# Moving four on-chip buffers from byte 16512 to a multiple of 4 KiB, in a kernel bound by its DMA engines

## Chip, cores, metric

One core of a Trainium2 chip. The metric is device time in microseconds (us) of one execution, the median of several. The profile's span, from the first to the last instruction, is some 1.4 us shorter than the time.

## The reference

```python
def setup_inputs():
    return {"x": np.random.randn(8192, 8192).astype(np.float32)}

def reference(x):
    a, b = np.split(x, 2, axis=-1)
    return a * (1 / (1 + np.exp(-b)))
```

268 MB are read and 134 MB written; each output needs one sigmoid and one product.

## The kernel before

The work goes through 32 tiles of 256 rows. Each of 128 partitions takes two adjacent rows (R = 2), so a partition's share of a load is one run of 65,536 bytes in HBM and on chip, and of a store one run of 32,768 bytes. Two input slots and two output slots take turns. Loads are issued by SyncE, stores by ScalarE; the sigmoid runs on ScalarE (ACT) in place, the product on VectorE (DVE).

```python
    pool = ctx.enter_context(tc.tile_pool(name="io", bufs=1))
    xs = [pool.tile([P, R * n_cols], fp32, name=f"x_sb{k}") for k in range(SLOTS)]
    os = [pool.tile([P, R * half], fp32, name=f"o_sb{k}") for k in range(SLOTS)]
    # ...
    for i in range(n_tiles):
        # ...
        rows = xs[i % SLOTS].rearrange("p (r h m) -> p r h m", r=R, h=2)
        packed = os[i % SLOTS].rearrange("p (r m) -> p r m", r=R)
        load = nc.sync.dma_start(out=xs[i % SLOTS], in_=x_t[i])
        # ... the first and last tile are worked in four parts, the others in one
        def store(cols):
            ins = nc.scalar.dma_start(out=out_t[i, :, cols], in_=os[i % SLOTS][:, cols])
            now["stores"].append(ins)
        for k, (r, c) in enumerate(parts):
            b = rows[:, r, 1, c]
            sig = nc.scalar.activation(out=b, in_=b, func=SIG)
            mul = nc.vector.tensor_mul(out=packed[:, r, c], in0=rows[:, r, 0, c], in1=b)
            # ... dependencies that follow from others are taken out
        store(chunks[-1] if i == n_tiles - 1 else slice(0, R * half))
```

The buffers are laid out one after another behind 16 KiB of scratch and four small constants. As built, they begin at bytes 16512, 82048, 147584 and 180352 of each partition.

## Time and profile before

| | before |
|---|---|
| time, median (range) | 933.2 us (933.03 to 933.31) |
| span of the profile | 931.7 us |
| DVE busy, ACT busy | 30%, 24% |
| DMA engines | full in all 40 slices, 432 GB/s |

To read such a page: look for the row that is full everywhere. Here it is the DMA row alone, and a change has to shorten what the DMA engines do, or it does nothing. The prediction below shows the lines.

This document also uses the records of single DMA packets, which the trace holds with start, duration, size and queue. A recorded duration is 3 to 4 ns longer than the time from one start to the next on the same engine; both forms occur below and are named.

### The profile page before, as it was taken

The numbers are of one execution on the slowest core, as the hardware profiler recorded it, in microseconds if no ns is written. First come the engines' busy times: TensorE is split into PE (matmuls) and PEld (weight loads), VectorE is DVE, ScalarE is ACT, GpSimd is POOL, SyncE is SP. The second block draws the span as 40 slices with busy tenths as digits, with TensorE's granted clock in tenths as the row PEclk, the third lists the DMA queues.
The fourth block names the chain that finished last, engine by engine and source line by source line (L and its number), as shares of the span: only waits on it lengthen the run. The fifth ranks groups of instructions, "written<-read, shape, count | busy, mean of one in ns | idle before, by whom it ended". The sixth has DMA issues, their size and how long they took to land.

```text
span 931.7 us, 247 instructions
## 1 busy us (share of the span) xinstructions
DVE 278.7 (30%) x38; ACT 227.1 (24%) x39; POOL 0.2 (0%) x4
## 2 busy tenths in 40 slices
DVE  0333213333133331233312333123331233312333
ACT  1323330233311333113331133311333113332033
POOL 0000000000000000000000000000000000000000
DMA  9999999999999999999999999999999999999999
GB/s 405 428 450 428 422 456 405 450 428 428 450 418 438 428 436 442 428 428 450 447 408 428 442 459 428 413 460 411 450 428 425 453 408 447 428 428 450 425 430 405
DMA packets 9649, 402.67 MB, mean 432 GB/s; under 512 B 1072, under 2 KB 1072, under 8 KB 1072
## 3 DMA queue, kind: packets, MB, share of 16 engines
q1 hardware_dynamic: 4608, 268.44, 66.6%
q10 hardware_dynamic: 5040, 134.22, 33.4%
q14 instruction: 1, 0.01, 0.0%
HBM read 268.44 MB, written 134.22 MB: 432 GB/s over the span
## 4 chain that ended last, share of the span: by engine, by line
DMA 73%; DVE 15%; ACT 12%; issue 0%; ACTq 0%
DMA x_sb<-in_x_dram 73%; DVE o_sb L69 15%; ACT x_sb L68 12%; ACTq L62 0%; ACTq L68 0%
## 5 line engine op out<-in xcount | busy, mean ns | idle before, releaser
L69 DVE TENSOR_TENSOR o_sb<-x_sb 128x8192 f32<-128x8192 f32 (+1 forms) x38 | 278.7, 7344 | 647.1 <-ACT x_sb L68 647.1
L68 ACT ACTIVATE x_sb<-x_sb 128x8192 f32<-128x8192 f32 (+1 forms) x38 | 225.8, 5952 | 695.6 <-DMA x_sb<-in_x_dram 694.4
L68 ACT ACT_TABLE_LOAD x1 | 1.3, 1283 | 0.8 <-PEq L188 0.8
L188 POOL MEMSET const-bfloat16-1.0<- 128x1 bf16 x1 | 0.1, 102 | 0.0
L188 POOL MEMSET const-uint8-127<- 128x1 uint8 x1 | 0.1, 102 | 0.0
L188 POOL MEMSET const-float32-0.0<- 128x1 f32 x1 | 0.1, 99 | 0.2 <-issue 0.2
L188 POOL MEMSET const-float32-1.0<- 128x1 f32 x1 | 0.1, 99 | 0.0
## 6 DMA issues: line engine op xcount, KB each, us to landing
out_dram<-o_sb ACTq DMA_DIRECT2D x31, 4096.0 KB, 34.7
out_dram<-o_sb ACTq DMA_DIRECT2D x4, 1024.0 KB, 5.6
x_sb<-in_x_dram SPq DMA_DIRECT2D x32, 42.2
```

The lines of the kernel that those rows point to most:

```text
L68: sig = nc.scalar.activation(out=b, in_=b, func=SIG)
L69: mul = nc.vector.tensor_mul(out=packed[:, r, c], in0=rows[:, r, 0, c], in1=b)
L188: nc = _bacc.Bacc("TRN2", target_bir_lowering=False, num_devices=1)
```

## The change

Its intent: DMA transfers might run faster when each partition's run begins on a round address, so a filler tile is put ahead of the four buffers.

```diff
     pool = ctx.enter_context(tc.tile_pool(name="io", bufs=1))
+    start = -(-nc.sbuf_base // 32) * 32
+    pool.tile([P, -start % (1 << 12) // 4], fp32, name="below")
     xs = [pool.tile([P, R * n_cols], fp32, name=f"x_sb{k}") for k in range(SLOTS)]
     os = [pool.tile([P, R * half], fp32, name=f"o_sb{k}") for k in range(SLOTS)]
```

The filler has 3968 bytes per partition. 16512 is 128 past a multiple of 256; the new start 20480 is 5 x 4096.

## The prediction

> **What bounds the kernel now.** I read the page first, then the DMA view, the table of stages, the waits of the load queue, the groups by shape and the chain of waits in order of time, and last the records of single DMA packets.
>
> The page shows two compute engines that idle most of the time and DMA engines that never do:
>
> ```profile
> span 931.7 us, 247 instructions
> DVE 278.7 (30%) x38; ACT 227.1 (24%) x39; POOL 0.2 (0%) x4
> DMA  9999999999999999999999999999999999999999
> DMA packets 9649, 402.67 MB, mean 432 GB/s; under 512 B 1072, under 2 KB 1072, under 8 KB 1072
> q1 hardware_dynamic: 4608, 268.44, 66.6%
> q10 hardware_dynamic: 5040, 134.22, 33.4%
> ```
>
> The DMA row is 9 in all 40 slices, and the shares of the two queues (loads on q1, stores on q10) add up to 100%. The table of stages says the same of two-tile stretches in the steady part and of the end (columns: stretch, busy time of DVE, ACT and POOL, clock, DMA share, GB/s):
>
> ```profile
> 102.88:160.84 57.96, 17.39 (x2) 14.06 (x3) 0.00 (x0) 1.00 1.00 432
> 160.84:218.77 57.93, 17.38 (x2) 14.06 (x2) 0.00 (x0) 1.00 1.00 434
> 914.71:931.70 16.99, 8.99 (x4) 7.54 (x4) 0.00 (x0) 1.00 0.94 401
> ```
>
> DMA share is 1.00 while DVE works 17.4 us and ACT 14.1 us of 58. Only in the last 17 us is a small part of the transfer time open.
>
> The chain of waits seems to tell another story, with compute on it:
>
> ```profile
> 102.88 7.04 ACT x_sb L68
> 109.94 8.70 DVE o_sb L69
> 118.66 42.09 DMA x_sb<-in_x_dram
> 160.84 7.04 ACT x_sb L68
> ```
>
> Each load waits for the multiplication that frees its slot. But the 15.7 us of ACT and DVE lie beside the other slot's load and the store before, as the share of 1.00 shows. A faster multiplication would only let a load enter the full queue earlier, and its 42 us would grow by as much. So the bound is the time that each DMA engine needs for its own packets.
>
> **What one packet costs.** The page counts 5040 + 4608 packets; the packet records show what they are: per load 128 of 65,536 bytes and 16 of 4 bytes (one per engine, the completion), per whole store 128 of 32,768 bytes and 16 of 4, per quarter store at the end 128 of 8,192 and 16 of 4. Following packets on one engine (each starts 3 to 4 ns before the recorded end of the last, so I lined them up by that), the time from one start to the next has hardly any spread: 2414.2 ns for a load packet, 1209.4 for a whole store packet, 305.9 for a quarter one, and 5.9 for a 4-byte one.
>
> The skill's page gives 32 bytes at 850 MHz per engine, 27.2 bytes per ns or 1.176 ns a beat. At that rate the data alone take 65,536/27.2 = 2409.4, 32,768/27.2 = 1204.7, 8,192/27.2 = 301.2 and one beat 1.2 ns. What is left is 4.8, 4.7, 4.7 and 4.7 ns: four beats, whatever the size, direction and kind.
>
> Sum for one of 16 engines: 256 x 2414.2 + 248 x 1209.4 + 32 x 305.9 + 67 x 5.9 ns = 618.0 + 299.9 + 9.8 + 0.4 = 928.1 us. The span is 931.7, so all that is not packets is 3.6 us: the start until the first load packet, the longer first packets and the gaps at the end.
>
> **What the Trainium skill says.** "DMA: Bandwidth & Descriptors", section "Where 436 GB/s comes from", has 16 ports x 256 bits x 850 MHz = 435.2 GB/s. The trace agrees: 432 over the span, so 99%. At 435.2 the 402.67 MB take 925.3 us (an estimate from that page's rate and this page's bytes), the least that any change of this kind can reach: 6.4 us or 0.7% below the profiled span.
>
> The same page, "How a descriptor splits into AXI transactions", is what the change bets on: a piece that does not start on a multiple of 256 bytes has its first transaction start at the boundary below, and the bytes before the start are fetched for nothing. Byte 16512 is 64 x 256 + 128, so a read from there would fetch 128 needless bytes, four beats of 32. That is exactly the excess found above, which makes the bet tempting. The section tells of reads alone; a store reads SBUF, a load writes it.
>
> The same page, "Why small descriptors are slow (HBM only)", has a rival for those four beats: a fixed overhead of about 3 cycles per packet on the engine's internal bus. The trace shows 4 for all four sizes. That includes the 4-byte completion packets, which move none of the tiles' data. I take this as the better fit: one cause explains all.
>
> "SBUF — State Buffer", section "Operand start alignment", asks only for a multiple of the element size and says that its runs timed nothing. So no page gives a speed for 4 KiB alignment.
>
> **The change part by part.** Removed: nothing. Added: a tile that no instruction reads or writes; it holds 3968 bytes per partition, costs no time, and still fits. Moved: the four buffers begin at 20480, 86016, 151552 and 184320 in place of 16512, 82048, 147584 and 180352, all higher by 3968. I compared the instructions of before and after engine by engine: same rows, same order, same shapes; only line and buffer numbers differ. Tile sizes and addresses in HBM stay.
>
> Distances between buffers stay too (65,536 and 32,768 bytes), so nothing that depends on how two buffers lie to one another can change.
>
> Compute: no gain, and it would not count.
>
> ```profile
> L69 DVE TENSOR_TENSOR o_sb<-x_sb 128x8192 f32<-128x8192 f32 x30 | 260.8, 8692 | 608.1 <-ACT x_sb L68 608.1
> L68 ACT ACTIVATE x_sb<-x_sb 128x8192 f32<-128x8192 f32 x30 | 210.9, 7031 | 652.8 <-DMA x_sb<-in_x_dram 652.8
> L69 DVE TENSOR_TENSOR o_sb<-x_sb 128x2048 f32<-128x2048 f32 x8 | 17.9, 2288 | 39.0 <-ACT x_sb L68 39.0
> L68 ACT ACTIVATE x_sb<-x_sb 128x2048 f32<-128x2048 f32 x8 | 14.8, 1903 | 42.9 <-DMA x_sb<-in_x_dram 41.6 <-DVE o_sb L69 0.9 <-issue 0.3
> ```
>
> From 2048 to 8192 columns DVE grows by 6404 ns for 6144 columns, 1.042 ns each, and ACT by 5128, 0.835 each; taken back to no columns both leave about 0.15 to 0.2 us. A straight line through both sizes shows no step an address could remove, and in the steady part both hide.
>
> Transfers: under the fixed-overhead reading all periods stay, so the sum stays 928.1 us and the change is 0. Sum of the parts: 0 us.
>
> **The rivals.** First, wasted beats at both ends of both directions: every data packet loses its four beats. 256 + 248 + 32 = 536 packets per engine x 4 x 1.176 ns = 2.5 us, all on the bound, giving 930.7 us (-0.27%). For it: the excess is four beats. Against it: 4-byte packets show the same four, and would need a second cause. Second, the store side only: 280 x 4.7 ns = 1.3 us, giving 931.9. Against it: loads and stores would then show different excesses unless something else adds four beats to loads; they show 4.8 and 4.7. Third, a slowdown, if a 4 KiB boundary makes all streams begin on the same place in the memory. Against it: the distances were multiples of 4 KiB before. To cross 2% it would have to add 18.7 us / 536 = 35 ns to every data packet, seven times the present excess. Nothing in the profile speaks for it. Fourth, the change of a wait: if landings moved, load issues could collide differently with stores; but with the queues never empty the sum of packets is what it is, so nothing below a microsecond changes.
>
> **Range and chances.** I give the fixed overhead about 85%, the two beat rivals together 12%, a slowdown 3%. Weighted: 933.2 - 0.08 x 2.5 - 0.04 x 1.3, so 932.9; I say 933.0. The three runs of before spread by 0.3 us; another session or chip can move both ends, so I allow 931.2 to 934.6, which leaves the whole-gain rival just outside. Faster by 2% would need 914.5 us, under the 925.3 us floor: 0.5%. Slower by 2%: 1.5%. Within 2%: 98%.
>
> **What would show it.** Right: data packets keep 2414, 1209 and 306 ns from start to start, DMA share stays 1.00 in the steady stretches, two-tile periods stay near 58.0 us, DVE and ACT means stay 8692 and 7031 ns. The beats rival: periods of about 2409.4, 1204.7 and 301.2 ns while the 4-byte packets keep 5.9, and two-tile periods shorter by 2 x 16 x 4.7 ns = 0.15 us. Store side only: 1204.7 beside an unchanged 2414. What would make me wrong: packet periods longer by tens of ns, or a DMA share below 1 in the steady part.

## The result, and the profile after

| | before | after |
|---|---|---|
| time, median of 5 (range) | 933.2 us (933.03 to 933.31) | 933.14 us (933.08 to 933.94) |
| ratio, 95% interval | | 0.9999 (0.9987 to 1.0011) |
| load packet, mean recorded duration | 2424.2 ns | 2424.9 ns |
| whole store packet | 1213.0 ns | 1213.0 ns |

The interval reaches down to 0.9987, a gain of 1.2 us, so the times alone only just exclude the smallest gain among the prediction's rivals (1.3 us); the packet times below decide it.

The page of the changed kernel, the lines that answer to those in the prediction:

```profile
span 932.6 us, 247 instructions
DVE 278.6 (30%) x38; ACT 227.0 (24%) x39; POOL 0.2 (0%) x4
DMA  9999999999999999999999999999999999999999
q1 hardware_dynamic: 4608, 268.44, 66.6%
q10 hardware_dynamic: 5040, 134.22, 33.4%
```

The profiled run happened to be the slowest of its five (933.94 us); the other four had spans of 931.7 to 932.1 us. What put it 0.9 us above the span of before was not followed up. Its table of stages in the same stretches (columns: stretch, busy DVE, ACT and POOL, clock, DMA share, GB/s):

```profile
102.88:160.84 57.96, 17.38 (x2) 14.06 (x2) 0.00 (x0) 1.00 1.00 434
160.84:218.77 57.93, 17.38 (x2) 14.06 (x2) 0.00 (x0) 1.00 1.00 434
914.71:931.70 16.99, 8.98 (x4) 7.53 (x4) 0.00 (x0) 1.00 0.94 403
```

And the two compute groups of whole tiles, by shape:

```profile
L71 DVE TENSOR_TENSOR o_sb<-x_sb 128x8192 f32<-128x8192 f32 x30 | 260.8, 8692 | 608.8 <-ACT x_sb L70 608.8
L70 ACT ACTIVATE x_sb<-x_sb 128x8192 f32<-128x8192 f32 x30 | 210.9, 7029 | 653.5 <-DMA x_sb<-in_x_dram 653.5
```

The DMA share stays 1.00, compute stays within 2 ns per instruction. In the packet records the commonest time from start to start is 2414 ns for a load and 1209 for a whole store, as before.

### The profile page after: what moved, and what is told of

It reads as the page before. It is cut to its first block, busy times and chain, and to the rows that moved or that the text cites. A ratio compares the mean times of both kernels' runs of the same rounds, so it can differ in the third digit from the quotient of the medians.

```text
span 932.6 us, 247 instructions
## 1 busy us (share of the span) xinstructions
DVE 278.6 (30%) x38; ACT 227.0 (24%) x39; POOL 0.2 (0%) x4
## 4 chain that ended last, share of the span: by engine, by line
DMA 73%; DVE 15%; ACT 12%; issue 0%; ACTq 0%
DMA x_sb<-in_x_dram 73%; DVE o_sb L71 15%; ACT x_sb L70 12%; ACTq L64 0%; ACTq L70 0%
```

## The experiments

A kernel that stays the same leaves two explanations: the address has no effect, or it has one that this kernel hides. With 536 data packets per engine, an effect of a few ns per packet is at the edge of what the measured times can tell. So I made the packets small. In the "small" kernels each partition's run goes in pieces of 4096 bytes: the two rows of a partition take turns on chip piece by piece, each row has its own DMA, and compute is as before.

```diff
-        rows = xs[i % SLOTS].rearrange("p (r h m) -> p r h m", r=R, h=2)
-        packed = os[i % SLOTS].rearrange("p (r m) -> p r m", r=R)
-        load = nc.sync.dma_start(out=xs[i % SLOTS], in_=x_t[i])
+        C = 4
+        # ... (lines cut here and below: a comment, an unused width, the declared dependencies)
+        rows = xs[i % SLOTS].rearrange("p (h c r w) -> p h c r w", h=2, c=C, r=R)
+        packed = os[i % SLOTS].rearrange("p (c r w) -> p c r w", c=C, r=R)
+        by_row = xs[i % SLOTS].rearrange("p (g r w) -> p g r w", g=2 * C, r=R)
+        x_ram = x_t[i].rearrange("p (r g w) -> p r g w", r=R, g=2 * C)
+        for r in range(R):
+            load = nc.sync.dma_start(out=by_row[:, :, r, :], in_=x_ram[:, r])
     # ... the stores likewise, one per row
```

That makes 6144 data packets per engine. Theory: four beats per packet, fixed, address without effect. Rival: the four beats come of the start at 16512. All medians and ratios in one place, the last column against the runs of before on the same chip:

| kernel | x, o bytes past a multiple of 256 | median us (range) | ratio |
|---|---|---|---|
| small_16512 | 128, 128 | 965.77 (965.70 to 965.86) | 1.0347 |
| small_20480 | 0, 0 (multiples of 4 KiB) | 959.61 (959.47 to 959.84) | 1.0281 |
| small_20704 | 224, 224 | 966.00 (965.88 to 966.12) | 1.0349 |
| small_20512 | 32, 32 | 966.05 (965.85 to 966.17) | 1.0350 |
| small_20736 | 0, 0 (not of 512) | 959.71 (959.54 to 959.90) | 1.0283 |
| small_x_off | 128, 0 | 965.89 (965.84 to 966.00) | 1.0350 |
| small_o_off | 0, 128 | 959.61 (959.59 to 959.67) | 1.0282 |
| small_20484 | each 4 past a multiple of 32, waits changed too | 1041.43 (1040.83 to 1041.67) | 1.1156 |
| small_x_4 | x 4 past a multiple of 32, waits changed too | 1033.43 (1033.20 to 1034.58) | 1.1075 |
| plain_20484 | each 4 past a multiple of 32, large packets | 933.57 (933.11 to 934.30) | 1.0005 |
| loads_16512 | 128, no stores | 653.87 (652.11 to 659.30) | 0.7017 |
| loads_20480 | 0, no stores | 653.74 (651.55 to 655.28) | 0.7003 |

All gave the right result but the two without stores. In the first seven the instructions and their waits are the same; only addresses differ.

### small_16512 and small_20480: packet cost, and the address

The second has this more:

```diff
+    start = -(-nc.sbuf_base // 32) * 32
+    pool.tile([P, (20480 - start) // 4], fp32, name="below")
```

> Every tile moves in pieces of 4096 bytes in place of 65,536 and 32,768, so the cost per packet counts 6144 times an engine in place of 536; buffers begin at 16512 as before. Fixed-overhead theory: 6144 x (150.6 + 4.7) ns = 954.1 us, completions 130 x 5.9 ns = 0.8, the 3.6 us at the ends and the 1.5 us between span and time: about 960 us (+2.9%), packet period 155.3 ns. Beats rival: the same here, since this base is 128 past a multiple of 256. If the four beats were per DMA or per byte and not per packet: about 934.

> The same pieces with the buffers moved to 20480, so that every piece begins on a multiple of 4 KiB. Fixed-overhead theory: as small_16512 within 0.2%, about 960 us, period 155.3 ns. Beats rival at both ends: all four beats of every packet go, 6144 x 4.7 = 28.9 us less, about 931. Beats on the store side only: 2048 x 4.7 = 9.6 us less, about 950, with store periods of 150.6 beside loads of 155.3.

The aligned one took 959.61 us where the fixed overhead asked for 960. Over the changed kernel that is 26.5 us (26.3 over the runs of before on the same chip), and 6144 - 536 = 5608 more packets at 4.7 ns make 26.4 (63 more completions make 0.4). Between 200 and 800 us of its packet records each engine starts a packet every 155.4 ns, completions included, where 155.3 was expected. So the four beats are a cost per packet, and alignment does not remove them: the beats rival, at 931 or 950 us, falls.

But small_16512 did not come out "within 0.2%": it is 6.2 us slower, 0.64%. The GB/s rows of the two pages (40 equal slices) show that the loss is not everywhere. First small_16512:

```profile
GB/s 381 421 410 421 420 416 422 414 422 421 416 421 416 421 421 416 421 416 421 421 417 421 416 420 421 418 420 417 420 421 418 420 417 420 421 418 420 418 419 402
```

Then small_20480:

```profile
GB/s 378 421 422 422 422 422 422 421 421 422 422 422 422 421 421 422 422 422 422 421 421 422 422 422 422 422 421 422 422 422 422 422 421 421 422 422 421 422 421 406
```

The aligned one is flat at 421 to 422; the other drops to 410 to 418 in some slices and returns. I marked each load packet as alone when no store packet starts within 300 ns of its time on any engine. After the first 45 us and before the last 30, alone packets of small_16512 have a mean recorded duration of 162.1 ns and the others 159.3; in small_20480 both have 159.0. The packets of the long stretches of loads alone, by time since the stretch began (mean recorded ns, from the packet records):

```
us into stretch   1.0   2.0   3.0   4.0   5.0   6.0   8.0  10.0  12.0
small_16512     159.3 159.4 160.7 160.6 162.5 163.6 163.9 164.1 164.1
small_20480     159.5 159.0 159.0 159.0 159.0 159.0 159.0 159.0 159.0
```

A misaligned load packet costs about 5 ns more, near the four beats again, but only once loads have been alone for some microseconds. Up to then something takes up the lag; adding up what the packets of the first 6 us fall short of 164 gives 0.1 to 0.15 us per engine (an estimate). The sum fits: the mean over all load packets is 160.8 against 159.3 ns, and 4096 load packets per engine x 1.5 ns = 6.1 us of the measured 6.2.

### small_20704, small_20512, small_20736: which offset counts

The filler of small_20480 with another end: 20704, 20512 and 20736 in place of 20480.

> The same pieces with the buffers at 20704, 224 bytes past a multiple of 256. Fixed-overhead theory: as small_16512, about 960 us. If a read that starts off a multiple of 256 fetches the bytes below for nothing (224 bytes, 7 beats of 1.18 ns), stores cost 8.2 ns more each than in small_20480: 2048 x 8.2 = 16.9 us, about 977 over a fixed 960. If writes waste them too: 6144 x 8.2 = 50.6 us, about 1010.

> Pieces of 4096 bytes with buffers at 20512: a multiple of 32, 32 bytes past a multiple of 256. Theory: as 16512 (128 past) and 20704 (224 past), about 966 us, the size of the offset not counting, since each piece crosses one 256-byte boundary more. Rival, the cost grows with the offset: a quarter of the 6.2 us, 961. Rival, what made 20484 slow is any small offset: 1041.

> Pieces of 4096 bytes, buffers at 20736: a multiple of 256 but not of 512 or 4096. Theory now: only a start off a multiple of 256 costs anything (16512 is 128 past one, 20704 is 224 past, both cost 6.2 to 6.4 us more than 20480): then this is as small_20480, 959.6 us, load packets at 159 ns in the records. Rival, 4 KiB or 512 bytes are what counts: about 966 as small_16512, with a quarter of the load packets at 160 to 172 ns.

Offsets of 32, 128 and 224 all cost the same 6.2 to 6.4 us, and 20736 = 81 x 256 costs nothing. So of the starts tried here only those on a multiple of 256 are free, 4 KiB is more than is needed, and the loss does not grow with the bytes before the start. A piece of 4096 bytes that begins off a multiple of 256 touches 17 blocks of 256 instead of 16; that one more block costs a fixed time fits the numbers, but no run shows the block itself. The expectation for 20704 that wasted beats add up to 977 or 1010 us was wrong.

### small_x_off and small_o_off: loads or stores

The misaligned half is chosen by a filler between the input and output buffers (small_o_off also has the filler below of small_20480).

```diff
+    pool.tile([P, 3968 // 4], fp32, name="between")   # x_off: x at 16512, o at 151552
+    pool.tile([P, 128 // 4], fp32, name="between")    # o_off: x at 20480, o at 151680
```

> Pieces of 4096 bytes; only the two input buffers begin at 16512 and 82048, the two output buffers at multiples of 4 KiB (151552, 184320). Theory now: the cost is on the writing of loads, in the stretches where loads run with no store beside them: 965.8 us as small_16512, slow load packets there and nowhere else. Rival, the reading of stores: 959.6. Rival, the distance between input and output buffers: neither of the two.

> The counterpart: input buffers at multiples of 4 KiB (20480, 86016), output buffers 128 bytes past one (151680, 184448). Theory now: reads of stores lose nothing, so 959.6 us as small_20480 and all packets at 159 ns. Rival, reads that begin below and are thrown away: 128 bytes are four beats, 2048 x 4.7 = 9.6 us more, or 6.2 if the loss of small_16512 was all theirs.

All of the loss is the loads', which write the on-chip memory. Stores that read it at 128 past a multiple of 256 lose nothing measurable: 959.61 us again. They run beside loads nearly all the time, which could hide a loss of theirs as stores hide the loads'. At the end they run alone: after the last load of small_16512 all of some 1,400 store packets, 14 us of them, are recorded at 159 ns, where loads alone had reached 164 within 6 us. In small_o_off 142 of some 1,100 are longer, most by a few ns. In small_20480, where everything is aligned, 28 are not at 159 either, and in small_20704 and small_20512, whose output buffers are off too, every one is at 159; so what lengthens those 142 stays open. The distance between input and output buffers, changed in both, plays no part.

### small_20484, small_x_4 and plain_20484: four bytes off

To begin 4 bytes past a multiple of 32, each buffer was a slice of a tile 32 bytes wider (in small_x_4 the input buffers only).

```diff
+    OFF = 1
-    xs = [pool.tile([P, R * n_cols], fp32, name=f"x_sb{k}") for k in range(SLOTS)]
+    xs = [pool.tile([P, R * n_cols + 8], fp32, name=f"x_sb{k}")[:, OFF : OFF + R * n_cols] for k in range(SLOTS)]
     # ... os likewise; the fillers are cut
```

> The same pieces, every buffer begins 4 bytes past a multiple of 32 (20484, 86052 and so on), so each piece of 4096 bytes touches 129 lines of 32 bytes in place of 128. Fixed-overhead theory, address without any effect: about 960 us. If a line of 32 bytes that is only partly used costs a beat of its own: 6144 x 1.18 = 7.2 us more, about 967, periods 156.5 ns; for stores alone 2.4 us more. If partly written lines must be read first, much more than that, on loads.

> Pieces of 4096 bytes, input buffers 4 bytes past a multiple of 32 (20484, 86052), output buffers at multiples of 4 KiB. If the 82 us of small_20484 come of loads that write parts of 32-byte lines: about 1041 again. If they come of stores that read them: 966, the 256-byte cost of the loads alone. If of both: between.

> The kernel with its large packets (65,536 and 32,768 bytes) and every buffer 4 bytes past a multiple of 32. Theory now: the cost is per packet and of some 4.8 ns, only when loads run alone, and large packets give it time to be made up: 933.2 us within 0.2%. Rival, the loss of small_20484 (82 us against 20480) is a cost per byte or per transfer of a 4-byte offset: about 1010. If it is a cost per packet: 82 us x 536/6144 = 7 us, about 940.

The two small ones are spoiled experiments. Their 1041 and 1033 us look like a huge price for four bytes, and I chose small_x_4 on that reading. The waits of the load queue point to the cause (columns: who waited for whom, us in total, times, longest). small_20480:

```profile
SPq L58 <- DVE o_sb L80: 576.0, 30, 20.6
```

small_20484:

```profile
SPq L59 <- DMA x_sb<-in_x_dram: 866.0, 32, 29.7
SPq L59 <- DVE o_sb L81: 95.5, 15, 22.1
```

The slice made the program order the two row loads of one buffer one after the other: 32 waits for an earlier load, 866 us in total, that the aligned kernel does not have. I compared the instructions after the fact and found that wait in the program itself. The packet records show its trace: in small_20484 no packet starts between 163 and 164 us, and those after the pause take up to 785 ns. But no run has these waits with aligned buffers, so how much of the 82 us they make is not shown, nor why small_x_4 is 8 us faster with nearly the same waits (858.8 us). So the times of these two say nothing clean about four bytes. Their packet records say a little: 6 to 13 us into a stretch of loads alone, load packets of both take 163.5 to 163.9 ns, as at the other offsets (164 in small_16512).

The large-packet kernel with the same slices has the waits of before. First before, then plain_20484:

```profile
SPq L50 <- DVE o_sb L69: 859.9, 30, 31.7
SPq L53 <- DVE o_sb L72: 859.8, 30, 31.7
```

It takes 933.57 us, ratio 1.0005 (0.9992 to 1.0017): with large packets, even a start that is off every multiple of 8 costs nothing measurable.

### loads_16512 and loads_20480: large packets without stores

Can large packets be made to show the cost? I left out all stores but the last tile's.

```diff
-        store(chunks[-1] if i == n_tiles - 1 else slice(0, R * half))
+        if i == n_tiles - 1:
+            store(chunks[-1])
```

> The kernel of before without its stores, but for the last tile's (a wrong result on purpose), buffers at 16512, so that loads of 65,536-byte packets run alone all the time. Theory: writing a packet that starts off a multiple of 256 takes some 4.8 ns longer at the memory, about 100 ns of that lag is absorbed first (some 20 packets), then each of the last 236 load packets takes 2419 ns from start to start in place of 2414 and the kernel about 1.1 us more than loads_20480; both near 640 us. Rival, large packets never lag: periods of 2414 throughout and no difference.

> The same without stores, buffers at 20480. Theory: 2414 ns from start to start for all load packets, some 1.1 us faster than loads_16512, about 639 us. Rival: equal to it.

Inconclusive. The medians differ by 0.1 us where single runs scatter by 4 to 7, and the median load packet is at 2418 recorded ns in both; the expected 2419 from start to start did not appear. The means do differ by 4.5 ns (2460.9 against 2456.4), but by the tail: some 9% of the packets are over 2500 ns, 392 against 362, and without them the order turns round (2420.7 against 2421.7). The chain of waits of loads_16512 shows a reason why the effect could not appear (pieces of 0.02 us are left out):

```profile
216.18 23.66 DMA x_sb<-in_x_dram
239.86 7.04 ACT x_sb L68
246.92 8.70 DVE o_sb L69
255.64 24.10 DMA x_sb<-in_x_dram
```

From one load of this slot to the next go 39.46 us, in which each engine moves two loads: 2 x 8 packets x 2414.2 ns = 38.6 us. So the engines pause some 0.4 us per load, far more than the 8 x 4.7 = 38 ns of lag that a load can build up. The pauses also explain most of why both took 654 us where about 640 was expected: 32 x 0.4 us are 13. A test of this needs loads that never pause, and more packets per stretch.

## Why the prediction was right, point by point

**The bound.** Confirmed: DMA share 1.00 and unchanged packet times before and after, compute unchanged.

**The four beats are a fixed cost per packet.** This carried the forecast, and it is now shown: 5608 more packets cost 26.5 us with every start aligned, against 26.8 worked out. Where the prediction inferred it from the 4-byte completions, the small kernels measured it. Where in the engine the cost arises, no run shows.

**The beats rivals.** Both fall as they were put: no packet time changed from before to after. The store-side one also fails where it would be amplified, in small_o_off.

**"Sum of the parts: 0 us."** Right in result, but the reading behind it, that a start address has no effect, was too wide, so the zero was partly luck (though the worst case below would still lie inside the stated range). Misaligned loads do cost about 5 ns per packet more; the prediction had not seen that this shows only where loads run alone, and none of its rivals put a cost on the loads alone, which is where it was. Why it does not show in this kernel can be read from the packet records of before. A load and a store of one tile have eight data packets each on an engine, 65,536 and 32,768 bytes, and the engine takes one from each queue in turn: 3392 of the 4096 load packets are followed directly by a store packet. The Trainium skill ("DMA: Bandwidth & Descriptors", section "Queues, rings and completion order") says that an engine goes round between its queues packet by packet; these records agree. So the two queues last equally long. Of 4096 load packets 224 run alone, all in the first 45 us before stores have begun, and none in the steady part (here alone means that no store packet starts within 1500 ns). Each load packet has a store packet of 1209 ns after it, in which a lag of 5 ns can be made up. In the small kernels a tile has 128 load packets against 64 store packets per engine, so stores run out first and 31,669 of 65,536 load packets of small_16512 are alone. That the lag is made up beside stores is what the 159 ns there show; where it waits is not shown. The 224 packets that run alone are 14 per engine, whose lag of 14 x 4.7 = 66 ns stays below the 0.1 to 0.15 us that was taken up first (both are estimates from the small kernels). So for large packets the hiding is argued from these figures; the runs without stores, which were to show it, did not.

The size it could have had at worst: 256 load packets x 4.7 ns = 1.2 us, 0.13%, had loads run alone throughout (an estimate from the small kernels' cost per packet).

**A slowdown.** None; the interval ends at 1.0011.

**Compute.** The instructions kept their times. But a straight line through two sizes could not show that there is no step, as the prediction has it: any two points lie on a line. What shows it is the comparison of before and after, 8692 ns in both.

## What to carry to other kernels

Before aligning a buffer, count the packets and ask whether the direction that suffers ever runs alone: here the cost was some 5 ns for each load packet that began off a multiple of 256 bytes, seen only after a few microseconds of loads without stores, so it was some 0.65% with 4096-byte pieces and nothing measurable with 64 KiB ones. Where it matters, 256 bytes were enough and 4 KiB brought no more; fewer, larger packets were worth 2.8%, far more than any alignment. To test an effect that is too small to time, multiply the events that carry it, and compare the waits of the test kernels before believing their times.

## What the Trainium skill lacked or had wrong

- "DMA: Bandwidth & Descriptors", section "How a descriptor splits into AXI transactions": it tells of reads that begin below their start. In these runs reads of the on-chip memory 128 past a multiple of 256 cost nothing measurable (959.61 us against 959.61), and it was writes that did, 6.2 us for 4096 packets per engine. The cost did not grow with the offset (965.8, 966.0 and 966.05 us at 128, 224 and 32), and the page lacks that the cost is hidden while stores run beside the loads (159 ns a packet, against 164 after 6 us alone).
- The same page, section "Why small descriptors are slow (HBM only)": about 3 cycles per packet; measured 4.0 beats (4.7 to 4.8 ns) for packets of 4, 8,192, 32,768 and 65,536 bytes, and 26.5 us for 5608 more packets of 4096.
- "SBUF — State Buffer", section "Operand start alignment", has no times. These runs add: with 64 KiB and 32 KiB per partition, starts at 16512, 20480 and 4 bytes past a multiple of 32 differ by less than 0.2% (intervals of the ratios end at 1.0011 and 1.0017); with 4096-byte pieces a start off a multiple of 256 costs some 0.65% on the input side.
